# Moving the matmul tiles of a two-layer decoder kernel to 128-byte positions in SBUF, with shared Newton scratch columns

## The chip, the core and the metric

The kernel runs on one NeuronCore of one Trainium2 chip. The metric is the device time of one execution in microseconds (us). Three executions before the change gave 597.43, 597.54 and 598.24 us; the median is 597.54 us. TensorE is called PE below, VectorE DVE, ScalarE ACT, GpSimd POOL, and SP is the engine whose queue issues nearly all DMAs. SBUF is the on-chip memory that all of these read: 128 partitions, in each of which a tile has a start position in bytes.

## The reference

The reference is a decoder trunk of two layers on 256 tokens with a model width of 1024, in float32.

```python
h = _rmsnorm(x, a_norm_attn[i]);  z = h @ a_w_in[i]                 # layer A
o_self = _diff_attention(q, k, v, lam, lam_init, a_subln[i])        # softmax - lam * softmax
o_mem  = _memory_attention(qm, mem, a_mem_norm[i], a_w_mem_kv[i])
x = x + concat([o_self, o_mem]) @ a_w_out[i]
x = x + _sq_relu_mlp(_rmsnorm(x, a_norm_mlp[i]), a_w_up[i], a_w_down[i])   # 1024 -> 4096 -> 1024
...                                                                 # layer B: the same with MoBA attention,
return _rmsnorm(x, final_norm)                                      # which at 256 tokens is one causal block
```

Nearly all arithmetic is in the products with the weights: 192 pieces of 128 rows by 1024 columns of float32 are read from HBM once each.

## The kernel before

**Precision.** Every weight product is made of three matmuls in the one-pass format float32r. A float32 operand `w` is split into a rounded part `wh` (ACT, L336) and the rest `wl = w - wh` (DVE, L338). The activations are split in the same way (L352 and L354 for the normalised `xn`). The product is then `wh*xh + wl*xh + wh*xl`. Each of these matmuls loads 128 columns of weights into the array (LDWEIGHTS, "PEld") and then streams 256 or 512 columns of the other operand through it.

**Stages.** Each layer has a mixer and an MLP. In the mixer, L499 computes projections into natural layout (512 streamed columns, the weights streaming and `xn` standing), then come scores, softmax and transposes (L557 to L740), then the output projection (L765, 256 streamed columns). In the MLP, L821 computes the up projection (256 streamed columns of `xn`, the weights standing) and L871 the down projection (512 streamed columns of weights, the activations standing). Six of each layer's sixteen pairs of down pieces use seven block products for eight (L894 to L921), which costs DVE work on `wsum`.

**Order of the work.** A planner in the kernel (class `Plan`) simulates the engines with fixed costs and writes each engine's order. All instructions of an engine go out in that written order; semaphores hold them back where data is not there yet. The planner knows nothing of addresses.

**Tiles in SBUF.** `fixed(...)` takes a tile from a pool of constants, in the order of the calls, each at the next multiple of 32 bytes. The ring pool (`w`, `wh`, `wl`, the large `B` tiles, `q`, `u`, and so on) starts where the constants end. All ring tiles are multiples of 128 bytes long, so they share one position modulo 128. The reciprocal square roots (`rsqrt`, `rsqrt_sum`) are Newton steps on DVE, on 1, 2 or 4 columns; each call takes scratch tiles `rst` and `rsq` of its own from the pool of constants, 18 of 32 bytes each.

Of the kernel before, what the change touches and what calls it, by code (L numbers as in the profile page):

```python
# [225 lines left out]
def tile_hybrid(ctx: ExitStack, tc: tile.TileContext, xa, xb, memt, xnat, mnat, w0, wall, consts, fgain, out):  # L226
# [13 lines left out]
    def name(s):  # L240
        uid[0] += 1
        return f"{s}_{uid[0]}"
# [15 lines left out]
    def fixed(shape, nm, dt=F32):  # L258
        return const.tile(shape, dt, name=name(nm))
# [2 lines left out]
    NG = len(GAINS) * KT  # L262
    xg = fixed([128, NG + KT * S], "xT")
    xT = xg[:, NG:].rearrange("p (k s) -> p k s", k=KT)
    xnt = fixed([128, KT, 2, S], "xn", F32R)
    g = {n: xg[:, i * KT:(i + 1) * KT] for i, n in enumerate(GAINS)}
    cst = fixed([128, 513], "consts")
# [9 lines left out]
    mv = fixed([128, 2, 4, 64], "mv")  # L277
    vb = fixed([128, 2, 12, 64], "vb")

    wsum = fixed([128, 2048], "wsum")  # L280


# [88 lines left out]
    def mem_tiles(gname):  # L371
# [11 lines left out]
                early("mem")(split_scaled)(lambda w=w, i=i: w.t[:, i], [w], g[gname][:, k:k + 1], T, k)  # L383
        return T

    def rsqrt(y, ms, n):

        t = fixed([128, n], "rst")
        q = fixed([128, n], "rsq")
        nc.vector.tensor_scalar(y.bitcast(I32), ms.bitcast(I32), -0.5, float(0x5F3759DF), op0=OP.mult, op1=OP.add)  # L390
        nc.vector.tensor_mul(t, y, y)
        nc.vector.tensor_mul(t, t, ms)
        nc.vector.scalar_tensor_tensor(q, t, -10.0 / 3.0, t, op0=OP.add, op1=OP.mult)
        nc.vector.scalar_tensor_tensor(y, q, 5.0, y, op0=OP.add, op1=OP.mult)

        nc.vector.scalar_tensor_tensor(t, y, -0.5 * 0.375 ** 2, y, op0=OP.mult, op1=OP.mult)
        nc.vector.tensor_mul(t, t, ms)
        nc.vector.tensor_scalar(t, t, 0.375, 1.5 * 0.375, op0=OP.mult, op1=OP.add)
        nc.vector.tensor_mul(y, y, t)

    def rsqrt_sum(y, s):

        t = fixed([128, 1], "rst")
        nc.vector.tensor_scalar(y.bitcast(I32), s.bitcast(I32), -0.5, float(0x5F3759DF), op0=OP.mult, op1=OP.add)
        nc.vector.scalar_tensor_tensor(t, y, s, y, op0=OP.mult, op1=OP.mult)
        nc.vector.scalar_tensor_tensor(t, t, -10.0 / 3.0, t, op0=OP.add, op1=OP.mult)
        nc.vector.scalar_tensor_tensor(y, t, 5.0, y, op0=OP.add, op1=OP.mult)
        nc.vector.scalar_tensor_tensor(t, y, s, y, op0=OP.mult, op1=OP.mult)
        f = 0.375 * D ** 0.5
        nc.vector.tensor_scalar(t, t, -0.5 * 0.375 ** 2 * f, 1.5 * f, op0=OP.mult, op1=OP.add)  # L410
        nc.vector.tensor_mul(y, y, t)

    class Stats:
# [10 lines left out]
        @early("stat")  # L424
        def whole(self, src, i):

            t = big(i, [128, 2, D])
            ss = fixed([128, 2, 2], "ss")
            cells = [(c, hf) for c in range(2) for hf in range(2)]
            dma(lambda: t.t, src, 1024 * CW, w=[(t, x) for x in cells])  # L430
            for c, hf in cells:
                def sq(c=c, hf=hf):
                    v = t.t[:, hf, c * 512:(c + 1) * 512]
                    nc.scalar.activation(v, v, AF.Square, accum_out=ss[:, c, hf:hf + 1])
                P.add(("act", t_act(512) + 100, sq), [(t, (c, hf))], [(t, (c, hf)), ("ss", id(ss), c, hf)])

            def emit():
                ms = fixed([128, 2], "ms")
                nc.vector.tensor_add(ms, ss[:, 0], ss[:, 1])
                nc.vector.tensor_scalar(ms, ms, 1.0 / D, EPS, op0=OP.mult, op1=OP.add)  # L440
                rsqrt(self.r, ms, 2)
                nc.vector.tensor_scalar_mul(self.r8, self.r, 0.125)
            P.add(("dve", 2250, emit), [("ss", id(ss), c, hf) for c, hf in cells], [self.key])
# [11 lines left out]
        def rstd(self):  # L455
            ps = bank("t")

            def mm():
                for h in range(2):
                    nc.tensor.matmul(ps.t[:, h:h + 1], self.acc.t[:, h * 128:(h + 1) * 128], ones[:, 0:1],  # L460
                                     start=h == 0, stop=True, skip_group_check=True)
            P.add(("pe", 220, mm), [self.acc], [ps])

            def emit():
                ms = fixed([128, 2], "ms")
                nc.vector.tensor_scalar(ms, ps.t[:, 0:2], 1.0 / D, EPS, op0=OP.mult, op1=OP.add)
                rsqrt(self.r, ms, 2)
                nc.vector.tensor_scalar_mul(self.r8, self.r, 0.125)
            P.add(("dve", 2100, emit), [ps], [self.key])
            return self  # L470
# [236 lines left out]
    def diff_out(prs, prl, v):  # L707
# [31 lines left out]
        def emit():  # L739
            nc.vector.tensor_scalar(ms, ms, 1.0 / 128, EPS, op0=OP.mult, op1=OP.add)  # L740
            rsqrt(rr, ms.rearrange("p a b -> p (a b)"), 2 * n)
# [256 lines left out]
    def mlp_last(st):  # L998
# [48 lines left out]
        for hf in range(2):  # L1047
# [32 lines left out]
            def rstd(ss=ss, part_=part_, r=r):  # L1080
                nc.vector.tensor_add(part_, part_, ss[:, 3:4])
                rsqrt_sum(r, part_)
# [319 lines left out]
```

## Time and profile before

| What | Value |
|---|---|
| Device time, median of 3 | 597.54 us (597.43 to 598.24) |
| Profiled execution, its span | 725.8 us; the page gives no other time for it |
| Mean granted TensorE clock in the profiled execution | 0.755 |
| PE busy | 716.6 us, 99% of the span, 3794 matmuls |
| DVE busy | 491.3 us, 68% |
| ACT busy | 398.0 us, 55% |
| HBM traffic | 148 GB/s over the span |

The profiled execution is 128 us longer than the timed ones. It ran at a granted clock of about 0.75 from its tenth microsecond on. Times of PE are therefore to be read with that clock; DVE, ACT and POOL do not follow it. A group row gives the source line, engine, operation, output and input tiles, sizes and count, then busy time, mean ns of one, and the idle time ahead of it. A row of windows gives the stretch, its length, the busy time of each engine with its instruction count, the granted clock, the DMA share and GB/s.

### The profile page before, as it was taken

Reading aid. Unit: us, or ns where it says so; the run is one execution under the profiler, and the core shown is the slowest. Engines: PE = TensorE matmul, PEld = TensorE weight load, DVE = VectorE, ACT = ScalarE, POOL = GpSimd, SP = SyncE. Lnnn points to the kernel's source line nnn. Section 1 sums busy time; section 2 is a strip of 40 time slices with the busy share of each in tenths; the row PEclk is TensorE's granted clock in tenths of the full one; section 3 lists DMA queues with packets and bytes.
Section 4 is the critical chain, followed back from the end, with each engine's and each line's share of the span. In section 5 each row is a group of like instructions: output and inputs, shape, how many; then the busy total and the mean of one; then the engine's idle time right before and its main releaser. Section 6 shows DMA issues by size and latency. Waiting matters only on the chain.

```text
span 725.8 us, 10368 instructions
## 1 busy us (share of the span) xinstructions
PE 716.6 (99%) x3794; PEld 590.5 (81%) x3794; DVE 491.3 (68%) x871; ACT 398.0 (55%) x750; POOL 54.4 (8%) x67
## 2 busy tenths in 40 slices
PE   9999999999999999999999999999999999999996
PEld 7676769999999977677777776889999999776775
DVE  5777666587556687766776577675675666876664
ACT  6776666455544554444575477656464455554422
POOL 0121110030000000000111121001200000000002
PEclk8777777777777777777777777777777777777777
DMA  8854432435444433546455432224444443354421
GB/s 303 293 183 165 146 95 79 145 119 175 151 168 146 152 139 132 188 145 209 139 174 179 169 120 85 88 88 143 153 164 152 154 158 125 127 186 151 148 85 59
DMA packets 30003, 108.45 MB, mean 149 GB/s; under 512 B 3328, under 2 KB 3328, under 8 KB 29696
## 3 DMA queue, kind: packets, MB, share of 16 engines
q1 hardware_dynamic: 29664, 107.26, 43.4%
q8 instruction: 30, 0.49, 0.3%
q10 hardware_dynamic: 288, 0.52, 0.2%
q14 instruction: 21, 0.17, 0.1%
HBM read 106.72 MB, written 1.05 MB: 148 GB/s over the span
## 4 chain that ended last, share of the span: by engine, by line
PE 98%; DVE 1%; DMA 1%; ACT 0%; issue 0%; SPq 0%; ACTq 0%
PE acc L821 30%; PE acc L499 23%; PE t L871 23%; PE acc L765 7%; PE acc L871 6%; PE t L586 2%; PE t L624 2%; PE t L681 1%; PE t L557 1%; DMA xT<-xa 1%; PE t L1013 0%; PE t L990 0%; DVE xT L751 0%; PE t L579 0%; PE t L721 0%; PE t L720 0%
## 5 line engine op out<-in xcount | busy, mean ns | idle before, releaser
L336 ACT CAST wh<-w 128x512 fp32r<-128x512 f32 (+1 forms) x232 | 182.5, 814 | 191.3 <-PE acc L821 74.0
L338 DVE TENSOR_TENSOR wl<-w,wh 128x512 fp32r<-128x512 f32 (+1 forms) x232 | 213.4, 939 | 86.7 <-ACT wh L336 71.7
L821 PE MATMUL acc<-xn,wh 128*128 128x256 f32 x1024 | 157.3, 314 | 0.5 <-DVE xn L354 0.5
L821 PEld LDWEIGHTS acc<-xn,wh 128*128 128x128 f32 x1024 | 150.7, 224 | 0.7 <-DVE xn L354 0.7
L871 PE MATMUL t<-wh,B 128*128 128x512 f32 (+1 forms) x368 | 134.4, 453 | 0.0
L499 PE MATMUL acc<-wh,xn 128*128 128x512 f32 x256 | 101.6, 472 | 0.7 <-ACT xn L352 0.7
L871 PEld LDWEIGHTS t<-wh,B 128*128 128x128 f32 x368 | 72.5, 199 | 29.8
L821 PE MATMUL acc<-xn,wl 128*128 128x256 f32 x512 | 84.1, 314 | 0.0
L871 PE MATMUL t<-wl,B 128*128 128x512 f32 (+1 forms) x184 | 82.9, 450 | 0.0
L821 PEld LDWEIGHTS acc<-xn,wl 128*128 128x128 f32 x512 | 78.1, 224 | 0.0
L499 PEld LDWEIGHTS acc<-wh,xn 128*128 128x128 f32 x256 | 51.0, 199 | 23.5 <-issue 2.2
L765 PE MATMUL acc<-B,wh 128*128 128x256 f32 x256 | 60.1, 323 | 0.0
L499 PE MATMUL acc<-wl,xn 128*128 128x512 f32 x128 | 58.0, 453 | 0.0
L790 DVE SCALAR_TENSOR_TENSOR u<-acc,rb 128x512 f32<-128x512 f32 x32 | 21.9, 690 | 50.5 <-PE acc L821 50.5
L871 PEld LDWEIGHTS t<-wl,B 128*128 128x128 f32 x184 | 37.0, 201 | 15.1
L765 PEld LDWEIGHTS acc<-B,wh 128*128 128x128 f32 x256 | 46.3, 216 | 0.9 <-issue 0.8
L452 POOL TENSOR_TENSOR sqa<-sqa,sq 128x256 f32<-128x256 f32 x21 | 20.3, 966 | 295.7 <-ACT sq L451 294.9
L765 PE MATMUL acc<-B,wl 128*128 128x256 f32 x128 | 40.0, 313 | 0.0
L895 DVE TENSOR_TENSOR wl<-wsum,wh 128x1024 fp32r<-128x1024 f32 x24 | 29.4, 1223 | 8.9 <-ACT wh L894 6.5
L533 POOL TENSOR_TENSOR ropet<-ropes,consts 128x256 f32<-128x256 f32 (+1 forms) x28 | 25.1, 917 | 129.0 <-ACT ropes L522 106.5
L499 PEld LDWEIGHTS acc<-wl,xn 128*128 128x128 f32 x128 | 26.8, 210 | 9.1
L894 ACT CAST wh<-wsum 128x1024 fp32r<-128x1024 f32 x24 | 25.3, 1052 | 15.9 <-PE acc L871 6.9
(223 smaller groups left out, 899.1 us busy)
## 6 DMA issues: line engine op xcount, KB each, us to landing
w<-wall SPq DMA_DIRECT2D x191, 512.0 KB, 3.3
w<-memt SPq DMA_DIRECT2D x4, 512.0 KB, 5.0
B<-xnat SPq DMA_DIRECT2D x1, 1024.0 KB, 7.4
B<-mnat SPq DMA_DIRECT2D x1, 1024.0 KB, 8.9
xT<-xa SPq DMA_DIRECT2D x1, 540.0 KB, 3.8
w<-w SPq DMA_DIRECT2D x2, 256.0 KB, 3.5
xT<-xb SPq DMA_DIRECT2D x1, 512.0 KB, 6.6
consts<-consts SPq DMA_DIRECT2D x1, 256.5 KB, 4.5
```

What stands on the lines that cost most here:

```text
L336: P.add(("act", t_act(n), lambda sl=sl: nc.scalar.copy(h.t[:, sl], w.t[:, sl])), [(w, x) for x in q], [(h, x) for x in q])
L338: P.add(("dve", t_dve(n), lambda sl=sl: nc.vector.tensor_sub(l.t[:, sl], w.t[:, sl], h.t[:, sl].bitcast(F32))), [(w, x) for x in q] + [(h, ...
L452: P.add(("pool", t_pool(S), lambda: nc.gpsimd.tensor_tensor(self.acc.t, self.acc.t, sq.t, op=OP.add)), [sq, self.acc], [self.acc])
L499: nc.tensor.matmul(pss[hf].t[:, c0:c1], a(k)[:, ts], b.t[:, o + c0:o + c1], start=(k == 0 and i == 0), stop=(k == KT - 1 and i == 2))
L533: nc.gpsimd.tensor_tensor(t.t[:, 0:nh, e:e + 32], zs.t[:, 0:nh, 32 - e:64 - e], b(sin[:, e:e + 32]), op=OP.mult)
L586: nc.tensor.matmul(sp[hd].t[:, c], qk[a].t[r, qb * 128:(qb + 1) * 128], qk[b].t[r, S:S + c.stop - c.start], start=(qb == 0 and i == 0 and ...
L765: nc.tensor.matmul(o, a.t[:, ws], x(k), start=(n == 0 and m % 2 == 0 and i == 0), stop=(n == KT - 1 and i == 2), skip_group_check=True)
L790: P.add(("dve", t_dve(512, True), lambda u=u, ps=ps: nc.vector.scalar_tensor_tensor(u.t, ps.t.rearrange("p (a s) -> p a s", a=2), 0.0, rb_ ...
L821: nc.tensor.matmul(ps.t[:, o], w.t[:, k * 128:(k + 1) * 128], xnt[:, k, x], skip_group_check=True, **flags)
L871: nc.tensor.matmul(ps.t[:, c0:c1], x, y, start=start and i == 0, stop=stop and i == 2, skip_group_check=True)
L894: P.add(("act", t_act(m), lambda: nc.scalar.copy(h[x].t[:, :m], src())), keys, [h[x]])
L895: P.add(("dve", t_dve(m), lambda: nc.vector.tensor_sub(l[x].t[:, :m], src(), h[x].t[:, :m].bitcast(F32))), keys + [h[x]], [l[x]], port=True)
```

## The change

There are two edits, and no instruction is added, removed or moved: on every engine the written order and the semaphore waits are the same as before.

- `rsqrt` and `rsqrt_sum` take their scratch tiles from a table with one entry for each width and name. 18 scratch tiles become 5, which frees 13 times 32 = 416 bytes per partition.
- Two tiles named `pad`, which nothing reads or writes, take 32 bytes ahead of `xn` and 96 bytes ahead of `wsum`.

In the built programs the tiles then stand so (byte position in the partition modulo 128):

| Tiles | before | after |
|---|---|---|
| `xn` (16 KB, both parts of the normalised activations) | 96 | 0 |
| ring: `w`, `wh`, `wl`, `B0` to `B7`, `qh`, `ql`, `u`, `o`, `sq`, ... | 32 | 0 |
| `ppx`, `mk`, `qm`, `mv`, `vb` | 32 | 64 |
| `wsum`, `ones` | 32 | 32 |
| `ident` (for the transposes) | 64 | 64 |

The ring ends at byte 229,280 before and at 228,992 after.

```diff
@@ -262,6 +262,7 @@
     xg = fixed([128, NG + KT * S], "xT")
     xT = xg[:, NG:].rearrange("p (k s) -> p k s", k=KT)
+    fixed([128, 8], "pad")
     xnt = fixed([128, KT, 2, S], "xn", F32R)
@@ -277,6 +278,7 @@
     vb = fixed([128, 2, 12, 64], "vb")
 
+    fixed([128, 24], "pad")
     wsum = fixed([128, 2048], "wsum")
@@ -383,10 +385,17 @@
+    shared = {}
+
+    def scratch(n, nm):
+
+        if (n, nm) not in shared:
+            shared[n, nm] = fixed([128, n], nm)
+        return shared[n, nm]
+
     def rsqrt(y, ms, n):
 
-        t = fixed([128, n], "rst")
-        q = fixed([128, n], "rsq")
+        t, q = scratch(n, "rst"), scratch(n, "rsq")
@@ -400,7 +409,7 @@
     def rsqrt_sum(y, s):
 
-        t = fixed([128, 1], "rst")
+        t = scratch(1, "rst")
```

## The prediction

> **What bounds the kernel now.** I read the granted clock first, then the page's busy times and its chain of waits, then the pace of single matmuls, and last the busy times by stage.
>
> ```profile
> core 0: 725.8 us, clock 0.755
> PE 716.6 (99%) x3794; PEld 590.5 (81%) x3794; DVE 491.3 (68%) x871; ACT 398.0 (55%) x750; POOL 54.4 (8%) x67
> PEclk8777777777777777777777777777777777777777
> PE 98%; DVE 1%; DMA 1%; ACT 0%; issue 0%; SPq 0%; ACTq 0%
> ```
>
> In the profiled execution PE is never free: it is busy for 99% of the span, and 98% of the chain that ended last is PE. But its clock was held at about three quarters. The timed executions took 597.54 us and the profiled one 725.8, so the timed ones cannot have run at this clock: 3794 matmuls need 716.6 us at it. The sum below has to be made for a faster clock than any row shows. That is the main difficulty here.
>
> The pace tells what a matmul costs. First a timeline of PE (start, length, line, operation, count), then the chain of waits (start, length, count):
>
> ```profile
> 6.58 1.05 PE L499 MATMUL acc<-wh,xn 128*128 128x512 f32 x2
> 7.43 0.63 PE L499 MATMUL acc<-wl,xn 128*128 128x512 f32 x1
> 7.86 1.05 PE L499 MATMUL acc<-wh,xn 128*128 128x512 f32 x2
> 8.71 0.63 PE L499 MATMUL acc<-wl,xn 128*128 128x512 f32 x1
> 9.14 1.05 PE L499 MATMUL acc<-wh,xn 128*128 128x512 f32 x2
> ```
>
> ```profile
> 165.47 91.95 PE acc L821 x648
> 307.63 7.65 PE t L871 x27
> ```
>
> - From 6.58 to 9.14 us six matmuls of 512 columns start, so one takes 2.56 / 6 = 427 ns.
> - In the down projection one of 512 columns takes 7.65 / 27 = 283.3 ns, at a granted clock of 0.75.
> - In the up projection one of 256 columns takes 91.95 / 648 = 141.9 ns, which is half of 283.3 (141.7).
>
> The cost per column is 0.553 ns in L871 and 0.554 in L821. So there is no fixed cost per matmul at this clock, and none for its position: in L821 the streamed operand `xn` stands at 96 and the weights at 32, in L871 both stand at 32. At a full clock the columns alone would take 283.3 * 0.75 = 212.5 ns for 512, which is 0.415 ns each.
>
> The busy times by stage (length, PE, PEld, DVE, ACT, POOL, granted clock, DMA share, GB/s):
>
> ```profile
> core 0: us, PE busy (x) PEld busy (x) DVE busy (x) ACT busy (x) POOL busy (x), PEclk, DMA share, GB/s
> 0.00:5.00 5.00, 3.81 (x34) 3.55 (x34) 1.46 (x6) 2.11 (x4) 0.44 (x5) 1.00 0.62 216
> 5.00:10.00 5.00, 4.45 (x11) 3.49 (x12) 3.72 (x8) 4.11 (x9) 0.00 (x0) 1.00 0.98 358
> ...
> 50.00:100.00 50.00, 50.00 (x226) 35.83 (x223) 37.39 (x94) 35.90 (x109) 6.92 (x8) 0.75 0.41 133
> ...
> 150.00:257.00 107.00, 107.00 (x756) 107.00 (x756) 70.72 (x109) 52.96 (x67) 5.59 (x5) 0.75 0.47 158
> 257.00:352.00 95.00, 95.00 (x342) 66.90 (x342) 69.17 (x85) 47.40 (x60) 0.00 (x0) 0.75 0.47 161
> ...
> 718.00:726.00 8.00, 0.87 (x7) 0.61 (x5) 2.91 (x12) 1.31 (x4) 0.20 (x1) 0.67 0.17 66
> ```
>
> Between 10 and 718 us PE is busy for 716.6 - 3.8 - 4.45 - 0.9 = 707.5 us. At a full clock that is 707.5 * 0.75 = 530.6 us. With the 10 us at the start and the 8 us at the end, 549 us is an estimate for an execution in which PE never waits. The timed 597.5 us lie 48 us above it. This surplus can be three things, which the profile cannot part: a clock of about 0.92 instead of 1; waits of PE for DVE and ACT; or a cost per matmul that the slow clock hides. For the second there is good reason: scaled to a full clock, PE would have 50 * 0.75 = 37.5 us of work in the stretch 50:100 against DVE's 37.4, and 71.3 against 69.2 in 257:352. In the up projection (150:257) PE leads clearly, 80.3 against 70.7.
>
> **The change part by part.** *Shared scratch.* No instruction and no wait is changed. Newton steps run one after the other on DVE, and each uses its scratch in that order alone. The cost is 0, with nothing that has to hide it; a gain is as little possible, since no duration depends on which of two columns is used.
>
> *Positions, for DVE, ACT and POOL.* The nearest rows are two of the same operation and size:
>
> ```profile
> L807 DVE TENSOR_TENSOR B<-u,B 128x512 fp32r<-128x512 f32 x32 | 21.9, 687 | 3.3 <-ACT B L805 3.3
> L921 DVE TENSOR_TENSOR xn<-vb,xn 128x512 fp32r<-128x512 f32 x6 | 4.1, 684 | 0.0
> ```
>
> L807 reads and writes tiles at 32; L921 reads at 32 and 96 and writes at 96. They take 687 and 684 ns. By these rows position does not matter to DVE, and I take 0. The bounds are 3 ns each way on 871 DVE instructions, 2.6 us, of which PE would see little.
>
> *Positions, for the DMAs.* DMA is at a share of 0.98 in 5:10 and at 0.41 to 0.47 in the later windows quoted. Only the first microseconds could feel a better write, and PE starts there on `xn` from `xa`. I take 0.
>
> *Positions, for PE.* This is the term on which the forecast rests. By the rows above a matmul costs its columns and nothing else at a granted 0.75, and just as little at the slower pace of the start: 427 / 283.3 = 1.51, which is 0.75 / 0.5. Those rows exclude a cost of position at these paces, but a cost that shows only when columns come faster than one in 0.553 ns is open. The bound below is found so: if SBUF hands over 128-byte pieces, or 32 columns, and a piece takes as long as 32 columns at a full clock (32 * 0.415 = 13.3 ns), then 512 columns from position 32 touch 17 pieces instead of 16 and take 225.8 ns instead of 212.5. Under the throttle 225.8 would be hidden behind 283.3. On all 3794 matmuls that is 3794 * 13.3 = 50 us, about the whole surplus of 48 us. The other end, a loss, is bounded under the rivals. Between the ends I take 0, because the nearest rows, two paces and two positions, all show 0.
>
> [...]
>
> Sum: 0 + 0 + 0 + 0. Against the profiled execution's own 725.8 us this leaves 725.8; against the median, 597.5 us. **Forecast: no change, 597.5 us.**
>
> **The rivals.** *A. Whole pieces, faster.* The mechanism is the one just priced. It would pay where PE leads, in the up projection and the output projection, whose 1024 + 512 + 256 + 128 = 1920 matmuls stand here:
>
> ```profile
> L821 PE MATMUL acc<-xn,wh 128*128 128x256 f32 x1024 | 157.3, 314 | 0.5 <-DVE xn L354 0.5
> L821 PE MATMUL acc<-xn,wl 128*128 128x256 f32 x512 | 84.1, 314 | 0.0
> L765 PE MATMUL acc<-B,wh 128*128 128x256 f32 x256 | 60.1, 323 | 0.0
> L765 PE MATMUL acc<-B,wl 128*128 128x256 f32 x128 | 40.0, 313 | 0.0
> ```
>
> 1920 * 13.3 = 25.5 us, so 572.0 us. In L499 and L871 DVE is within 3% of PE at a full clock, and what PE gains there it would wait for DVE. For it speaks that the surplus and the bound are of a size; against it, that DVE's waits and a lower clock explain the surplus as well.
>
> *A2. Half pieces, faster.* With pieces of 64 bytes, or with half of each piece hidden by reading ahead, the price is 6.7 ns, or 12.8 us on the same 1920: 584.7 us. [...] Such partial gains are the larger part of the faster cases.
>
> *B. Streams in step, slower.* PE reads a streamed operand and the next weights at once. Before, `xn` stands 64 bytes apart from `wh` and `wl` modulo 128; now they stand at the same place. If SBUF is divided into banks by the low address bits, the two reads of L821 (1536) and of L499 with `xn` (256 + 128) now begin on one bank. I price a collision at up to 16 bytes, 4 columns, 4 * 0.415 = 1.66 ns: 1920 * 1.66 = 3.2 us, or 600.7 us. The lines that would carry it in L499:
>
> ```profile
> L499 PE MATMUL acc<-wh,xn 128*128 128x512 f32 x256 | 101.6, 472 | 0.7 <-ACT xn L352 0.7
> L499 PE MATMUL acc<-wl,xn 128*128 128x512 f32 x128 | 58.0, 453 | 0.0
> ```
>
> It decides from 0.6 ns per matmul on (1.2 us / 1920). For it: in 150:257 the weight loads are busy for all of the 107 us, so both reads always run. Against it: L871, whose two operands both stand at 32 already, goes at the pace of L821, whose operands stand apart.
>
> *C. The change does not do what it says.* `ident`, `wsum`, `mk`, `qm`, `mv` and `vb` still stand off 128, but they carry few matmuls; the tiles of L499, L765, L821 and L871 all move. This would give the forecast's time, and has no chance of its own.
>
> **How the numbers follow.** A measurement of this kernel can tell about 0.2% from no change, 1.2 us. I give the forecast 0.43, A 0.12, A2 and smaller gains 0.29, and B 0.16. Faster is 0.41, the same 0.43, slower 0.16. The forecast's own range is 596.3 to 598.7. The range for 8 in 10 goes down past A2's 584.7 to 582, which leaves out A, and up to 601, just past B's 600.7, which leaves out a few hundredths for larger collisions.
>
> **What would show it.** If the forecast is right, the profile after shows the same paces (283 ns and 142 ns at 0.75), the same DVE rows and a span of 725.8 within 1 us. That alone does not prove it: A would leave a throttled profile just as unchanged, and shows only in the timed runs, or in a profile whose granted clock is near 1, where L821 would go below the pace of the kernel before. B would show as more than 141.9 ns in L821 with L871 unchanged. The forecast is wrong if the timed median leaves 596.3 to 598.7; its step "Positions, for PE" then failed, unless L807 and L921 moved as well.

## The result, and the profile after

The changed kernel takes 605.61 us (604.79 to 607.06), the kernel before 597.48 us in the same measurement: a ratio of 1.0137, with a 95% interval of 1.0106 to 1.0169. It is 8.1 us slower, where no change was forecast.

The profile shown before the prediction had been taken at a granted clock of 0.755. The one of the changed kernel was taken at 0.998, so the two cannot be set side by side. The kernel before was therefore run again; its profile at 0.996 is the one compared with here. Between the two, PE's busy time fell from 716.6 to 583.6 us, while those of DVE (491.3 and 485.1), ACT (398.0 and 390.7) and POOL (54.4 and 56.2) stayed within 4%. One execution of a later kernel, the one called half apart, took 973.23 us at a clock of 0.559 and counts in no ratio. First the spans and clocks, PE's busy row and the chain, of the kernel before (run again):

```profile
core 0: 595.2 us, clock 0.996
PE 583.6 (98%) x3794; PEld 515.1 (87%) x3794; DVE 485.1 (82%) x871; ACT 390.7 (66%) x750; POOL 56.2 (9%) x67
PE 88%; DVE 4%; ACT 3%; DMA 3%; issue 1%; SPq 0%; ACTq 0%
```

and of the changed kernel:

```profile
core 0: 605.2 us, clock 0.998
PE 591.4 (98%) x3794; PEld 522.7 (86%) x3794; DVE 485.0 (80%) x871; ACT 390.3 (64%) x750; POOL 55.9 (9%) x67
PE 87%; DMA 5%; DVE 4%; ACT 3%; issue 1%; SPq 0%; ACTq 0%; DVEq 0%
```

The span grew by 10.0 us, PE's busy time by 7.8 us, with the same number of instructions. The busy times of DVE, ACT and POOL stayed within 0.4 us. At a clock near 1 PE is still busy for 98% of both spans, so hardly anything hides a slower matmul.

Which matmuls became slower is seen in the groups. Before (run again):

```profile
L821 PE MATMUL acc<-xn,wh 128*128 128x256 f32 x1024 | 128.2, 277 | 1.1 <-DVE xn L354 1.1
L821 PE MATMUL acc<-xn,wl 128*128 128x256 f32 x512 | 69.1, 277 | 0.0
L871 PE MATMUL t<-wl,B 128*128 128x512 f32 (+1 forms) x184 | 71.0, 386 | 0.0
```

After (the line numbers are 9 higher):

```profile
L830 PE MATMUL acc<-xn,wh 128*128 128x256 f32 x1024 | 134.6, 284 | 1.0 <-DVE xn L356 1.0
L830 PE MATMUL acc<-xn,wl 128*128 128x256 f32 x512 | 72.3, 283 | 0.0
L880 PE MATMUL t<-wl,B 128*128 128x512 f32 (+1 forms) x184 | 71.0, 386 | 0.0
```

The up projection of the two MLPs took 9.6 us more (6.4 + 3.2); the down projection did not change. The pace is best read from the chain of waits, where each layer's up projection has one unbroken stretch of 648 matmuls (start, length, line, count). Before (run again):

```profile
141.78 73.45 PE acc L821 x648
431.50 73.46 PE acc L821 x648
```

After:

```profile
143.23 77.75 PE acc L830 x648
437.39 77.75 PE acc L830 x648
```

A matmul of 256 streamed columns started every 73.45 / 648 = 113.3 ns before, and every 77.75 / 648 = 120.0 ns after. On all 1536 matmuls of L821 that would be 1536 * 6.64 ns = 10.2 us; the groups say 9.6 us. Either is about the growth of the span, though not all of that growth lies in the matmuls: layer A's stretch already starts 1.5 us later (143.23 against 141.78). The timed difference is 8.1 us. The two profiles differ by more because the changed kernel's was taken of its slowest execution (607.06 us) and that of the kernel before of one below its median (596.99 of 597.77).

### The profile page after: what moved, and what is told of

Same layout as the page of the kernel before. It is cut to its first block, busy times and chain, and to the rows that moved or that the text cites. A ratio compares the mean times of both kernels' runs of the same rounds, so it can differ in the third digit from the quotient of the medians.

```text
span 605.2 us, 10368 instructions
## 1 busy us (share of the span) xinstructions
PE 591.4 (98%) x3794; PEld 522.7 (86%) x3794; DVE 485.0 (80%) x871; ACT 390.3 (64%) x750; POOL 55.9 (9%) x67
## 4 chain that ended last, share of the span: by engine, by line
PE 87%; DMA 5%; DVE 4%; ACT 3%; issue 1%; SPq 0%; ACTq 0%; DVEq 0%
PE acc L830 30%; PE t L880 22%; PE acc L508 14%; PE acc L774 7%; PE acc L880 6%; DMA w<-wall 3%; PE t L595 2%; PE t L633 2%; PE t L690 1%; DVE wl L340 1%; DMA w<-memt 1%; ACT wh L338 1%; PE t L566 1%; DMA xT<-xa 1%; ACT wh L354 0%
## 5 line engine op out<-in xcount | busy, mean ns | idle before, releaser
L830 PE MATMUL acc<-xn,wh 128*128 128x256 f32 x1024 | 134.6, 284 | 1.0 <-DVE xn L356 1.0
L830 PEld LDWEIGHTS acc<-xn,wh 128*128 128x128 f32 x1024 | 127.8, 192 | 1.5 <-DVE xn L356 1.2
L880 PE MATMUL t<-wh,B 128*128 128x512 f32 (+1 forms) x368 | 111.9, 386 | 0.0
L508 PE MATMUL acc<-wh,xn 128*128 128x512 f32 x256 | 84.9, 399 | 1.7 <-ACT wh L338 1.0
L880 PEld LDWEIGHTS t<-wh,B 128*128 128x128 f32 x368 | 68.6, 188 | 13.8
L830 PE MATMUL acc<-xn,wl 128*128 128x256 f32 x512 | 72.3, 283 | 0.0
L880 PE MATMUL t<-wl,B 128*128 128x512 f32 (+1 forms) x184 | 71.0, 386 | 0.0
L830 PEld LDWEIGHTS acc<-xn,wl 128*128 128x128 f32 x512 | 66.2, 192 | 0.0
L774 PE MATMUL acc<-B,wh 128*128 128x256 f32 x256 | 50.8, 289 | 0.0
L802 ACT ACTIVATE u<-u 128x512 f32<-128x512 f32 x32 | 20.1, 632 | 17.3 <-DVE u L799 17.1
L614 ACT ACTIVATE B<-t,nm 128x128 f32<-128x128 f32 (+1 forms) x64 | 27.1, 439 | 4.6 <-DVE nm L610 2.5
```

What stands on the lines that cost most here:

```text
L508: nc.tensor.matmul(pss[hf].t[:, c0:c1], a(k)[:, ts], b.t[:, o + c0:o + c1], start=(k == 0 and i == 0), stop=(k == KT - 1 and i == 2))
L614: nc.scalar.activation(p[hd].t[:, c], sp[hd].t[:, c], AF.Exp, bias=nm[hd][:, qb:qb + 1], accum_out=ss[:, hd, qb:qb + 1])
L774: nc.tensor.matmul(o, a.t[:, ws], x(k), start=(n == 0 and m % 2 == 0 and i == 0), stop=(n == KT - 1 and i == 2), skip_group_check=True)
L802: P.add(("act", t_act(512), lambda u=u: nc.scalar.activation(u.t, u.t, AF.Square)), [u], [u])
L830: nc.tensor.matmul(ps.t[:, o], w.t[:, k * 128:(k + 1) * 128], xnt[:, k, x], skip_group_check=True, **flags)
L880: nc.tensor.matmul(ps.t[:, c0:c1], x, y, start=start and i == 0, stop=stop and i == 2, skip_group_check=True)
```

## The experiments

All whole kernels below keep the order and the waits of the change; only positions differ. "Ring" is the position of `w`, `wh`, `wl` and the `B` tiles. "Pace" is that of the two 648-matmul stretches.

| Run | xn mod 256 | ring mod 256 | ring minus xn, mod 256 | us (median) | ratio to before, 95% | pace, layers A and B, ns |
|---|---|---|---|---|---|---|
| before, again | 96 | 160 | 64 | 597.77 | 0.9986 [0.9956, 1.0015] | 113.3, 113.4 |
| the change | 128 | 128 | 0 | 605.61 | 1.0137 [1.0106, 1.0169] | 120.0, 120.0 |
| shared scratch alone | 96 | 32 | 192 | 604.72 | 1.0102 [1.0069, 1.0136] | 117.8, 117.8 |
| ring at 0 | 96 | 0 | 160 | 607.79 | 1.0148 [1.0100, 1.0195] | 120.0, 120.0 |
| half apart | 192 | 128 | 192 | 604.24 | 1.0097 [1.0069, 1.0125] | 117.8, 117.8 |
| as before modulo 256 | 96 | 160 | 64 | 596.97 | 0.9989 [0.9976, 1.0002] | 113.3, 113.4 |
| after plus 64 | 128 | 192 | 64 | 602.89 | 1.0084 [1.0066, 1.0102] | 117.8, 117.8 |
| 0 and 64 | 0 | 64 | 64 | 599.94 | 0.9972 [0.9941, 1.0004] | 113.3, 117.8 |
| output apart | 96 | 160 | 64 | 595.97 | 0.9941 [0.9908, 0.9974] | 113.4, 113.4 |

The ratios are to the kernel before in the same measurement: 597.48 us for the change, 598.04 for the first set, 597.86 for the second. The last two rows were measured on another chip than these two sets, beside 600.29 us of the kernel before, so they are to be compared by the ratio.

### First set: the kernel before again, the scratch alone, and two other distances

The kernel before, again, has no edit.

> This is the kernel before, unchanged, run again so that its pace can be read at a clock near 1. In the changed kernel at a clock of 0.998 a matmul of 256 columns starts every 120 ns in the up projection and one of 512 every 227 ns in the down projection. Theory 1 (phase: a matmul costs more when its streamed operand and its weights stand at the same position modulo 128): the up projection, where xn stood at 96 and the weights at 32, goes at 114 to 115 ns (8.1 us / 1536 matmuls = 5.3 ns less), the down projection, where both stood at 32, at 227 ns as after. Theory 2 (absolute: tiles at a multiple of 128 bytes are slower wherever the other operand stands): both are faster than after, by about 8.1 us over 3246 matmuls, 2.5 ns: 117.5 and 224.5 ns. Theory 3 (the shared scratch or a changed wait costs the time): both paces as after, and PE shows more waits after than before. Time in all three 597.5 us.

It gave 597.77 us and a pace of 113.3 ns, near the 114 to 115 of theory 1. PE's idle time is 11.6 us before and 13.8 after, too little a difference for theory 3, and the down projection's rows are the same, so theories 2 and 3 were already in trouble.

Shared scratch alone:

```diff
-    fixed([128, 8], "pad")            # ahead of xn
-    fixed([128, 24], "pad")           # ahead of wsum
+    fixed([128, 8], "pad")            # ahead of mask_b, the last large constant
```

> The scratch is shared as in the change, but one pad of 32 bytes ahead of the ring is all that is left of the pads, so that xn stands at 96 and the ring at 32 modulo 128, as before. Theories 1 and 2: 597.5 us, within 1.2. Theory 3: 605.6 us.

604.72 us: theory 1, in its form modulo 128, and theory 2 fell, and theory 3 seemed to hold. But its profile shows the time not in Newton steps but in matmuls again, at a pace between the two seen so far:

```profile
140.88 76.32 PE acc L829 x648
434.86 76.32 PE acc L829 x648
```

76.32 / 648 = 117.8 ns. Modulo 128 all tiles of the matmuls stand as before; modulo 256 the ring does not (32 instead of 160).

No pad at all, which leaves the ring at 0:

```diff
-    fixed([128, 8], "pad")            # ahead of xn
-    fixed([128, 24], "pad")           # ahead of wsum
```

> The scratch is shared and no pad is there: xn stays at 96 as before, the ring goes to 0, as after. The two are 96 (or 32) bytes apart modulo 128. Theory 1, if only the same place costs: 597.5 us and 114 to 115 ns in the up projection; if the cost falls with the distance up to 64: between, near 601 us and 117 ns. Theory 2: most operands stand at 0, so the weights' share is paid: about 603 to 605 us.

607.79 us, the slowest of all, at 120.0 ns. None of the three expectations fits. Half apart:

```diff
-    fixed([128, 8], "pad")            # ahead of xn
+    fixed([128, 24], "pad")
-    fixed([128, 24], "pad")           # ahead of wsum
+    fixed([128, 8], "pad")
```

> Shared scratch, pads of 96 and 32 bytes: xn at 64, the ring at 0, so that the two are 64 bytes apart modulo 128 as before, while the ring is at a multiple of 128 as after. Theory 1: 597.5 us, up projection at 114 to 115 ns. Theory 2: 603 to 605 us, since the weights, which are most operands, stand at 0 as after, and only xn does not.

604.24 us. Theory 1's number was missed, and theory 2's hit for a wrong reason, as the pace shows: it is the same as in the run with the scratch alone, though there both tiles stand elsewhere.

```profile
141.42 76.32 PE acc L830 x648
435.34 76.32 PE acc L830 x648
```

The two have one thing in common: the ring stands 192 bytes behind `xn` modulo 256. That gave the next theory: the distance counts, with a period longer than 128 bytes.

### Matmuls alone: two maps

A kernel with nothing but one tile x, one tile w and matmuls. Its core:

```diff
+    for i in range(64):
+        o = 8 * i                      # 32 bytes further
+        for k in range(8):
+            for x in range(2):
+                nc.tensor.matmul(ps[:, 0:256], W[:, o + 128 * k:o + 128 * k + 128], X[:, k, x], ...)
+        for k in range(8):
+            nc.tensor.matmul(ps[:, 0:256], W[:, o + 128 * k:o + 128 * k + 128], X[:, k, 0], ...)
```

> A kernel of matmuls alone; everything else of the computation is left out and the output is meaningless. In one tile x of the size and layout of xn and one tile w of weights, both float32r, PE runs the 24 matmuls of one up-projection piece (128 weight columns, 256 streamed columns) 64 times, each time with the weights 32 bytes further from x: distances 0 to 2016 bytes modulo 4096. Then it runs 12 matmuls of 512 streamed columns in the order of the projections, again at 64 distances. In the whole kernels the distance of the weight tiles from xn modulo 2048 was 1088 (before: 113.6 ns for 256 columns), 704 (shared scratch alone and half apart: 117.8), 768 (after: 120.0) and 672 (ring at 0: 117 and 122 in turn, mean 120.0). Theory 1b (the cost comes from the distance between the two operands that PE reads at once, modulo more than 128 bytes): the map gives the same four numbers at the same four distances, with no other engine at work. Theory 4 (the cost comes from other engines or DMAs writing near the operands): the map is flat, near 109 to 114 ns.

The spacing of matmuls 3 to 23 of each group, from their starts, in ns by the distance in bytes (first row 0 to 224, next row 256 to 480; the six rows after these repeat the second within 0.1):

```
  0: 120.0 118.2 117.8 117.2 118.7 120.1 117.8 117.8
256: 119.7 118.2 117.8 117.2 118.7 120.1 117.8 117.8
```

In steps of 32 bytes the period is 256. The values at 0 (120.0), 160 (120.1) and 192 (117.8) are those of the whole kernels within 0.4 ns, with no other engine and no DMA at work. So the cost arises in PE's own work, from where the two operands that it reads stand, and theory 4 falls. But at 64 the map has 117.8 where the kernel before has 113.3. The second map takes x and w through all eight positions each:

```diff
+    for i in range(8):
+        for j in range(8):
+            ...                        # X[:, 8 * i + ...] and W[:, 8 * j + ...]
```

> Matmuls alone again, all else left out and the output meaningless. The map over the distance alone repeats every 256 bytes and gave 119.7 ns at 0, 120.1 at 160 and 117.8 at 192, as in the kernels after, ring at 0 and half apart, but 117.8 at 64 (1088), where the kernel before has 113.6. In that map x stood at 128 modulo 256, in the kernel before xn at 96. Now x and w both go through all eight positions of 32 bytes modulo 256, 64 pairs, in both patterns. Theory 1c (what counts is both positions modulo 256): the pair x at 96 and w at 160 gives 113 to 114 ns, the pairs of the other kernels (96, 32), (128, 128), (96, 0) and (192, 128) give 117.8, 120, 120 and 117.7. Theory 1b (the distance alone): all pairs at one distance are equal, and none comes below 117.

The timeline of that run (start, length, operation; the first letter after "up" is x's position, the second w's: a = 128, b = 160, c = 192, e = 0, f = 32, g = 64, h = 96 modulo 256):

```profile
24.28 2.99 PE L261 MATMUL upac<-x,w 128*128 128x256 f32 x24
27.11 2.98 PE L261 MATMUL upad<-x,w 128*128 128x256 f32 x24
...
120.83 3.04 PE L261 MATMUL upee<-x,w 128*128 128x256 f32 x24
123.71 3.00 PE L261 MATMUL upef<-x,w 128*128 128x256 f32 x24
126.55 2.90 PE L261 MATMUL upeg<-x,w 128*128 128x256 f32 x24
129.29 3.04 PE L261 MATMUL upeh<-x,w 128*128 128x256 f32 x24
...
180.52 2.91 PE L261 MATMUL uphb<-x,w 128*128 128x256 f32 x24
183.26 3.04 PE L261 MATMUL uphc<-x,w 128*128 128x256 f32 x24
```

From one start to the next, x at 0 and w at 0 need 2.88 us for 24 matmuls, 120.0 ns each. 0 and 64 need 2.74 us, 114.2 ns with the change of group in it (113.5 within), and so do 96 and 160, the positions before. But 128 and 192, at the same distance of 64, need 2.83 us, 117.9 ns. All four pairs of the slower kernels gave what was expected: 117.8, 120.0, 119.8 and 117.8. Five of the eight pairs at distance 64 gave 117.8 and one 117.6, only two 113.5 and 113.6. So either the two positions fix the pace, or there are two steady rhythms at one distance, and what ran before chooses. In this map the distance of 96 also had two values: 117.2 or 117.3 at six pairs, but 120.0 right behind the two pairs that had run at 113.5. That speaks for the second reading.

### Second set: the positions of before, the distance of 64 elsewhere, and finer steps

As before modulo 256, with shared scratch:

```diff
-    fixed([128, 8], "pad")            # ahead of xn
-    fixed([128, 24], "pad")           # ahead of wsum
+    fixed([128, 40], "pad")           # ahead of mask_b
```

> The scratch is shared as in the change; the pads are replaced by one of 160 bytes behind the other constants, ahead of the ring. xn then stands at 96 and the ring at 160 modulo 256, exactly as before; against the run with shared scratch alone (604.7 us) only the ring moves, by 128 bytes, which changes nothing modulo 128. Theory 1c (the positions of xn and the weights modulo 256 count): 597.5 us, within 1.2, and 113.3 ns for 256 columns in the up projection. Theory 3 (the shared scratch costs the time): 604 to 606 us and, since Newton steps cannot slow a matmul, 113.3 ns with more waiting. A rule modulo 128: 604.7 us and 117.8 ns.

596.97 us and 113.3 ns. Against the run with shared scratch alone, only the ring moved, by 128 bytes. The shared scratch is thereby cleared, and so is any rule modulo 128.

```profile
140.72 73.45 PE acc L829 x648
430.44 73.46 PE acc L829 x648
```

The changed kernel plus 64 bytes ahead of the ring:

```diff
+    fixed([128, 16], "pad")           # ahead of mask_b; the change's two pads stay
```

> The changed kernel with both its pads and 64 bytes more behind the other constants, ahead of the ring: xn stays at a multiple of 128 as after, the ring goes from 128 to 192 modulo 256, so that the weights stand 64 behind xn as before. Theory 1c, if the distance decides: 113.3 ns and 597 to 599 us. In the map of matmuls alone the distance of 64 gave 113.5 at two of eight positions and 117.8 at the others (x at 128 among these), as if PE could settle in either of two rhythms; if the position decides between them: 117.8 ns and 604 us. Theory 2 (multiples of 128 are bad or good as such): no change from after for xn, 120 ns.

602.89 us. It went at 117.8 ns for nearly all of the stage, but not from its start. The chain:

```profile
129.39 7.42 PE acc L831 x63
137.15 4.59 PE acc L831 x38
142.18 76.32 PE acc L831 x648
```

The 63 matmuls of the first line, with the small pauses that they hold, take 7.42 us; in the kernel before they take 7.43, in the run half apart, which goes at 117.8 ns, 7.69. Behind the second line the stage runs at 117.8 ns to its end. The fast rhythm exists at these positions, but it did not last.

The kernel before holds both rhythms too. Eight short matmuls break its up projection, four of L460 behind the 82nd matmul and four of L479 behind the 120th. From its timeline (run again):

```profile
132.85 1.98 PE L821 MATMUL acc<-xn,wh 128*128 128x256 f32 x16
134.66 1.07 PE L821 MATMUL acc<-xn,wl 128*128 128x256 f32 x8
136.25 0.50 PE L460 MATMUL t<-ones,sqa 128*128 128x1 f32 x4
137.16 2.05 PE L821 MATMUL acc<-xn,wh 128*128 128x256 f32 x16
139.05 1.10 PE L821 MATMUL acc<-xn,wl 128*128 128x256 f32 x8
141.17 0.60 PE L479 MATMUL t<-dg,ones 128*128 128x128 f32 x4
```

Ahead of the first break 16 matmuls take 134.66 - 132.85 = 1.81 us, 113.1 ns each. Between the breaks they take 139.05 - 137.16 = 1.89 us, 118.1 ns each, and behind the second the 648 run at 113.3. So at fixed positions the rhythm changed at a short interruption and changed back at the next; in the changed kernel plus 64 it stayed at 117.8 behind the second break.

Matmuls alone in finer steps, each group behind one at distance 0:

```diff
+    for i in range(64):
+        up("ra" + letters(i), 0)
+        up("up" + letters(i), i)      # 4 bytes further
+    for i in range(32):
+        down("rb" + letters(i), 0, 1)
+        down("dn" + letters(i), 2 * i, 3)
```

> Matmuls alone, all else left out, the output meaningless: the distance of the weights from x goes through 0 to 252 bytes in steps of 4 for the pattern of the up projection, and in steps of 8 for that of the projections with 512 columns; ahead of each stands the same pattern at distance 0 (24 and 3 matmuls), so that each begins in the same rhythm. If the bank of SBUF that an operand's next bytes lie in decides, with banks of 64 bytes and a period of 256: levels that change near multiples of 64, 120 near 0, 113.3 or 117.8 near 64, and no level below 113 anywhere. [...] 512 columns: the lowest, 226.7, at 0, as the weights and B tiles stand already.

```profile
111.62 2.99 PE L259 MATMUL upaq<-x,w 128*128 128x256 f32 x24
114.45 3.04 PE L259 MATMUL raar<-x,w 128*128 128x256 f32 x24
...
128.77 2.89 PE L259 MATMUL upat<-x,w 128*128 128x256 f32 x24
131.50 3.04 PE L259 MATMUL raau<-x,w 128*128 128x256 f32 x24
...
294.34 2.88 PE L259 MATMUL upbw<-x,w 128*128 128x256 f32 x24
297.06 3.04 PE L259 MATMUL rabx<-x,w 128*128 128x256 f32 x24
```

"aq" is a distance of 64 bytes: 2.83 / 24 = 117.9 ns. "at" is 76 bytes: 2.73 / 24 = 113.8 (113.3 within the group). "bw" is 192 bytes: 2.72 / 24 = 113.3. At 192 every pair of the second map and both whole kernels had gone at 117.8. The expected levels with steps at 64 bytes did not come: the values jump between 113.3 and 123.2 from one step of 4 bytes to the next. What held is that nothing went below 113.3, and that 512 columns have their lowest, 226.7 ns, at distance 0; all other distances lay between 230.0 and 235.3 here (in the first map the distance of 64 had 228.9).

### Third set: does the pair fix the rhythm, and a version that uses the finding

0 and 64:

```diff
-    fixed([128, 8], "pad")            # ahead of xn
+    fixed([128, 40], "pad")
-    fixed([128, 24], "pad")           # ahead of wsum
+    fixed([128, 40], "pad")           # ahead of mask_b
```

> Shared scratch, pads of 160 bytes ahead of xn and 160 behind the other constants: xn stands at 0 and the ring at 64 modulo 256, 64 bytes apart. In the map of matmuls alone this pair gave 113.5 ns, like 96 and 160, while 128 and 192 gave 117.8, as the run with the changed kernel's pads and 64 bytes more did. If the two positions modulo 256 fix the rhythm: 113.3 ns in the up projection and 597 us. If the rhythm depends on what ran before, so that the pair of the map was chance: 117.8 ns and 603 us, or a mix of both through the stage.

599.94 us, and the answer to the question stands in one profile:

```profile
143.53 73.45 PE acc L830 x648
433.32 76.32 PE acc L830 x648
```

With the same tiles at the same positions, layer A's up projection went at 113.3 ns and layer B's at 117.8. The positions allow the fast rhythm but do not fix it. One stage in the slower rhythm would cost 768 * 4.4 ns = 3.4 us. The times of this kernel run from 595.74 to 601.72 us, and the profile is of the slowest. The rhythm is only half of what makes it slow: its span is 5.8 us above that of the run as before modulo 256 (599.9 against 594.1), of which 2.8 us were lost before layer A's stretch began (143.53 against 140.72). No run was made on that early loss.

The last kernel moves `B0` and `B1`, which hold the mixer's output, to 64 bytes ahead of the weights:

```diff
     def big(i, shape, dt=F32):
-        return buf(f"B{i}", shape, dt)
+        if i > 1:
+            return buf(f"B{i}", shape, dt)
+        gap, at = ((48, 48), (16, 0))[i]       # 192 bytes ahead of B0, 64 behind B1
+        ...
+            t = ring.tile([128, 2048 + gap], dt, ...)
+            return t[:, at:at + 2048].rearrange(...)
```

> The run with shared scratch and the positions of before (597 us), with one thing more: B0 and B1, which hold the mixer's output for the output projection, are moved to 96 modulo 256, 64 bytes ahead of the weights at 160, where xn stands for the up projection. Theory 1c: the output projection, whose operands stood at one place, goes from 119.5 ns to 113.3 for 384 matmuls, 2.4 us less, if PE settles in the fast rhythm, or to 117.8, 0.7 us less, if not; in the down projection a quarter of the standing operands (B0 and B1 of eight) go from 226.7 to 228.9 ns, some 0.4 us more. 595 to 597 us. If positions do not matter for this pattern: 597 us and 119.5 ns.

595.97 us, against 600.29 for the kernel before in the same measurement, a ratio of 0.9941 [0.9908, 0.9974]. The output projection of layer B, as before modulo 256 and then with the move:

```profile
403.36 10.26 PE acc L773 x84
```

```profile
403.68 9.74 PE acc L782 x84
```

It goes from 122.1 to 116.0 ns per matmul, pauses included. In the groups the 384 matmuls' busy time falls from 50.8 + 36.1 to 49.3 + 35.6 us, by 2.0 us, near the 2.4 expected. That is a third of a per cent. The whole profiled execution shows no gain, first as before modulo 256, then with the move:

```profile
core 0: 594.1 us, clock 0.998
core 0: 594.2 us, clock 0.998
```

Nor can the rest of the ratio be put down to the move: in that measurement the kernel before scattered from 595.93 to 603.92 us, while this one had eight of its twelve times between 594.98 and 596.18. It was 0.6% faster than the kernel before in the same measurement. That it is better than the run as before modulo 256, which was timed on another chip, is not shown.

## Why the prediction was wrong, point by point

- **What bounds the kernel.** PE, as read. But of the three readings of the 48 us of surplus, the one for which it saw good reason, that PE waits for DVE and ACT, was wrong in the main. At a clock of 0.996 PE is busy for 583.6 of 595.2 us. Most of the surplus is a cost per matmul that the slow clock hid: 113.3 ns for 256 columns, where the scaled pace of 141.9 * 0.75 gives 106.4, and 226.7 for 512 in the map, where it gives 212.5.
- **Shared scratch, cost 0.** Right. The Newton step of L392 takes 160 to 161 ns on each of its five two-column scratch tiles before, and the same on the one tile after (L401). The run with shared scratch and the old positions modulo 256 has the old time.
- **Positions for DVE, ACT and POOL, 0.** Right: the row of L807 reads 687 ns on L816 after as well, and DVE's busy time is 485.0 against 485.1 us. For the DMAs no run was made. Their share of the chain reads 3% before and 5% after, but 3% as well in the slowest kernel, the ring at 0.
- **Positions for PE, 0.** This is the step that failed: the new positions cost L821 6.6 ns per matmul, 120.0 against 113.3. The prediction took 0 "because the nearest rows, two paces and two positions, all show 0". Those rows were taken at a mean spacing of 141.9 and 283.3 ns or slower; the cost of position lies between 113.3 and 120.0 ns and does not show in those means. The second pace speaks as little: the 0.5 in "0.75 / 0.5" stands in no row (that of 5:10 reads 1.00). That such a cost "is open" was said, and the 0 was then chosen by rows that could not speak. The range was too narrow as well: it took 0.2% as noise, while the kernel before itself later ran from 595.62 to 603.92 us.
- **A and A2.** Their sign was wrong, and that their sizes come near is chance. By A, tiles off the multiple of 128 would need 119.7 ns for 256 columns and 225.8 for 512; 120.0 and 226.7 were measured with all tiles on it. The pieces of 128 and of 64 bytes in their prices were suppositions; no run shows them. With xn at 96 and the ring at 160, both off it, the pace was 113.3.
- **B, streams in step, 0.16.** Right in its place and sign: L821, where `xn` and the weights came to stand together; L871, with both at one place before and after, unchanged. Its rule, the same place modulo 128, was not: with the shared scratch alone the two stand 64 bytes apart modulo 128 as before, and L821 ran at 117.8 ns. The price was too small by a factor of four: 1.66 ns was taken as the bound, 6.6 ns were measured. No run shows the banks it supposes or the 16 bytes from which that price is worked out. The term of L499 was wrong outright; its longest stretch does not slow down. Before (run again), then after:

```profile
322.49 21.99 PE acc L499 x96
```

```profile
328.04 21.93 PE acc L508 x96
```

That the pace depends on where PE's two operands stand is shown, by moving the ring alone by 128 bytes (117.8 to 113.3 ns) and by kernels with matmuls alone. That the same positions can run in two rhythms is shown as well. Why 256 bytes, and what chooses the rhythm at an interruption, stays open; no run here looked into the memory. That the slower timed runs of the kernel before, up to 603.92 us, are such a change of rhythm would fit the 3.4 us per stage, but no profile caught one, and the first 140 us, which differ by up to 2.8 us between the profiles shown, are a rival that no run parted from it.

## What to carry to other kernels

The profile at a clock of 0.755 showed 141.9 ns per matmul of 256 columns and hid a cost that stands between 113.3 and 120.0 ns at 0.996 and 0.998. Before pricing an edit on PE from such a profile, get one at the clock of the timed runs, and do not fill the gap with rows that cannot see it. Here PE was busy for 98% of the span and streamed float32r, and an edit that only moved tiles slowed the up projection by 5.9% (113.3 to 120.0 ns); sharing the scratch columns, with the tiles that moved by it, by 3.9% (to 117.8). So note the positions modulo 256 of the two operands of the heaviest matmul, and look at its spacing in the trace before and after. The times of the kernel 0 and 64 run from 595.74 to 601.72 us, and its one profile holds 113.3 ns in layer A and 117.8 in layer B; by the estimate of 3.4 us per stage, two rhythms can be part of such a scatter. A single profile shows only what ran in that execution.

## What the runs showed of the hardware

- No steady stretch of float32r matmuls on 128 rows went below 113.3 ns for 256 columns and 226.7 ns for 512 at a granted clock near 1: twice the columns, twice the time, 6 to 7% above 106.4 and 212.5 ns, the paces at the clock of 0.75 (141.9 and 283.3) scaled by it.
- Each float32r matmul left one record in the trace (1536 of L821 before, for 1536 instructions), each float32 matmul of layer A's scores two (64 of L586 for 32).
- In the long stretches of the up projection the mean spacing for 256 columns was 113.3, 117.8 or 120.0 ns; matmuls alone, in steps of 4 bytes, gave many more values, up to 123.2. Which one comes depends on the distance of streamed operand and weights, in steps of 32 bytes with a period of 256, but not on it alone: at the distance of 64 bytes the pace switched between 113.3 and 117.8 ns at short interruptions.
- The position of the weights alone changes the pace: moving only the ring, and with it the weights, by 128 bytes while `xn` stayed where it was changed both stretches of 648 matmuls from 117.8 to 113.3 ns. Where the two reads meet is not shown.
- For 512 streamed columns the order is reversed: the lowest, 226.7 ns, is at distance 0, where 256 columns have about 120.0. No distance measured here had the lowest of both.
